# Down projection of a fused encoder block as seven half-size products, with tokens stationary and weight sums made in DRAM

## The chip, the core and the metric

The kernel runs on one core of a Trainium2 chip, alone. Its time is the device time of one execution in microseconds (us), as the median of several runs. A core has five engines that each work through their own list of instructions in order: TensorE (PE, matmuls, with its weight loads shown as PEld), VectorE (DVE), ScalarE (ACT), GpSimd (POOL) and SyncE (SP, which here only issues transfers). Engines wait for one another through semaphores. SBUF is the on-chip memory with 128 partitions, PSUM the accumulator memory that PE writes, in banks of 128 x 512 fp32 numbers; DRAM is reached by DMA alone, which 16 DMA engines carry out. DMAs are issued by SP, ACT or POOL, each on a queue of its own.

## The reference: what is computed

One encoder block for 512 tokens of width 1024, all in float32: three token mixers, a gated merge, an output projection, a convolutional gated feed-forward network and a last RMSNorm. The change touches the last two:

```
def rms_norm(x, g):
    y = x * rsqrt(mean(x * x, axis=-1) + EPS)
    return y * g

def conv_glu_ffn(h, w_up, w_conv, b_conv, w_down):
    a, u = split(h @ w_up, 2)                       # 512 x 2816 each
    return (gelu(dwconv3(a, w_conv, b_conv)) * u) @ w_down   # 2816 x 1024

x = x + merged @ w_out
x = x + conv_glu_ffn(rms_norm(x, ffn_norm_g), ...)
return rms_norm(x, final_norm_g)
```

The down projection is (512 x 2816) @ (2816 x 1024).

## The kernel before

**Numbers in two parts.** Each fp32 matrix is split into a high part h (rounded to the fp32r format by an ACT copy) and a rest l (a DVE subtraction). A product then is three matmuls into the same PSUM bank, `mm3` (L212): h·h, h·l and l·h. Activations are split by `split_act` (L217; ACT L219, DVE L220), weights by `emit_split` (L176; ACT L195, DVE L196).

**The weight stream.** All weights lie in one flat DRAM array in the order of use (`block_list`, L63), in blocks of up to 128 x 1024 numbers (512 KB). `weights(key)` (L201) issues the DMAs of blocks up to three ahead on SP (L159, three `raw` buffers) and the splits of blocks up to one ahead, in halves of at most 512 columns, into four `hi` and four `lo` buffers, and hands out the slices. A high half can be overwritten as soon as PE has used what was in its buffer; so an ACT copy L195 often waits for PE, and the rest L196 waits for it.

**Activations transposed.** Nearly all projections hold activations with features on partitions and tokens along the free axis: the weight slice of 128 x 128 is stationary, the 512 tokens move. `proj` (L409) computes one tile of 128 output features x 512 tokens with 8 x 3 matmuls. Some early projections (L524, and the memory values at L1061) have it the other way: 128 tokens are stationary and up to 512 weight columns move.

**Order.** A tile framework takes the program order as priority, places each engine's instructions statically and adds the semaphores. Between the stages of the big projections (`xaq`, `o`, `memk`, `memv`, `naq`, `nak`, then the merge gates) generators for the mixers are advanced by `step`; one of them raises row sums to the power -1/2 on POOL (L756), which DVE needs at once (L759). From the merge gates on, POOL issues window loads for the neighbourhood attention (L552). `late` holds work that the next `proj` emits after its second k (`flush`, L404).

**The feed-forward part** runs in two halves of 11 feature tiles each (L1296). For each feature tile f: `proj` of the gate part `ua` (48 matmuls for `ua` and `uu` together), `conv` (L466: DVE L470, ACT L472, DVE L473 and L474), gelu (ACT L1320, DVE L1321, ACT L1322, DVE L1323, POOL L1324), `proj` of `uu`, their product on DVE (L1327, which waits for POOL), and its split into two parts (L1328). After each half the down projection adds its share to the residual `x2` (features on partitions): 8 tiles of 11 x 3 matmuls of 512 tokens in the first half, with a DVE add out of PSUM (L1334). The second half has five such tiles; in its last tiles (`last_tiles`, L1166) the remaining work is ordered so that the norm of the first 256 tokens, of token tile 2 and of token tile 3 can be finished one behind the other: tiles of 256 tokens, then two products with tokens stationary over the last 256 features, with small fp32 matmuls and transposes between them. The norm's sums are taken over partitions with matmuls against ones. The results leave in three outputs (`outa`, transposed; `outb`; `outc`), which the host puts together.

Of the kernel before, what the change touches and what calls it, by code (L numbers as in the profile page):

```python
# [26 lines left out]
LF = KT - 2  # L27
# [34 lines left out]

def block_list():  # L63
# [35 lines left out]
for _i, (_k, _n) in enumerate(BLOCKS):  # L99
    BINDEX[_k] = (_i, _off, _n)  # L100
    _off += P * _n
WTOTAL = _off
BCOLS = {n: (lambda k: P) for n in ("mlk", "o", "xaq", "memk", "naq", "nak", "g", "out", "ua", "uu", "dn")}
BCOLS.update({n: (lambda k: 512) for n in ("mlq", "memv")})
BCOLS["tm"] = lambda k: TMC[k[1]]
BCOLS["br"] = lambda k: 256
BCOLS["dnl"] = lambda k: 256
# [3 lines left out]
def hybrid_block(ctx, tc, xg, xT, memT, wflat, vecs, gbias, nabias, outa, outb, outc):  # L111
# [33 lines left out]

    raws, split = {}, {}
# [3 lines left out]
    def emit_raw(i):  # L150
# [7 lines left out]
        src = wflat[off:off + P * n].rearrange("(p n) -> p n", p=P)  # L158
        SY.dma_start(r[:, :n], src)  # L159
# [6 lines left out]

    lw = []

    def lastw(k, m):

        if not lw:
            lw.extend(unit(F32R) for _ in range(4))
        q = slice(k % 8 * 256, k % 8 * 256 + m)
        return lw[k // 8][:, HI256:][:, q], lw[2 + k // 8][:, q]

    def emit_split(i):  # L176
# [4 lines left out]
        for a, b in hs:  # L181
            m = (b - a) * c
            if key[0] == "dnl":
                h, l = lastw(4 * key[1] + a, m)
            else:
                h = wp.tile([P, HWT], F32R, tag="hi", name=nm("wh"), bufs=4)
                l = wp.tile([P, HWT], F32R, tag="lo", name=nm("wl"), bufs=4)
                if key[:2] == ("tm", 2):
                    h = h[:, HI256:]
# [34 lines left out]
    gbf = cp.tile([P, 272], F32, name="gbf")  # L224
    gb, gfin = gbf[:, :16], gbf[:, 16:]
# [234 lines left out]
    SY.dma_start(gbf, gbias.partition_broadcast(P))  # L460
# [572 lines left out]
    for f in range(4):  # L1033
# [12 lines left out]
        V.tensor_scalar(so[0][:, f * S:(f + 1) * S], t, 1.0, None, op0=ALU.add)  # L1046
        step(RB)
    mkv = unit()
    mk, mv = mkv[:, 0:1024], mkv[:, 1024:2048]
    for f in range(4):  # L1050
        ps = proj(("memk", f), MH, ML, M)
        V.tensor_tensor(mk[:, f * M:(f + 1) * M], ps[:, :M], mrb, op=ALU.mult)
        step(RM)
    pss = [mmps() for _ in range(2)]
    for i in range(4):
        ws = weights(("memv", i))
# [10 lines left out]
    for f in range(4):  # L1067
        ps = proj(("naq", f), XH, XL)
        V.tensor_tensor(nq[:, f * S:(f + 1) * S].rearrange("p (b r c) -> p b r c", r=ROWS, b=4), rv(ps), rv(rb),
                        op=ALU.mult)  # L1070
        step(RB)
    for f in range(4):
        ps = proj(("nak", f), XH, XL)
        V.scalar_tensor_tensor(nk[:, f * S:(f + 1) * S], ps, 0.125, rb, op0=ALU.mult, op1=ALU.mult)
        step(RB)
# [79 lines left out]
    acc3 = cp.tile([P, S], F32, name="acc_3", tag="acc", bufs=1)  # L1155
    x2v = [u[:, :4 * S].rearrange("p (f s) -> p f s", f=4) for u in x2u]

    Hf = S // 2
    half = {}

    def power(v):
        col = tiny(v.shape[-1])
        G.tensor_tensor(col, v, nhalf[:, :v.shape[-1]], op=ALU.pow)
        return col

    def last_tiles(U, UL_):  # L1166

        ws = [w for i in range(3) for w in weights(("dnl", i))]  # L1170
        w5 = weights(("dn", 1, LF - 1, 0)) + weights(("dn", 1, LF - 1, 1))

        def half_tile(f, cs, at={}):
            ps = mmps()[:, :Hf]
            fs = slice((f - LF) * P, (f - LF + 1) * P) if f >= LF else slice(0, P)
            for k in range(HF):
                w = ws[k] if f >= LF else w5[k]
                mm3(ps, w[0][:, fs], w[1][:, fs], U[k][:, cs], UL_[k][:, cs], k == 0, k == HF - 1)
                if k in at:
                    at[k]()  # L1180
            xf = x2[f][:, cs]
            V.tensor_tensor(xf, ps, xf, op=ALU.add)
            sq = scr(Hf)
            A.activation(sq, xf, AF.Square)
            V.tensor_tensor(acc3[:, cs], acc3[:, cs], sq, op=ALU.add)
            A.activation(xf, xf, AF.Copy, scale=vcol("fin_g", f))

        for f in range(LF - 1, KT):
            half_tile(f, slice(0, Hf))

        def cols_a():
            ps = atps()
            for t in range(2):
                PE.matmul(ps[:, t:t + 1], acc3[:, t * P:(t + 1) * P], ones[:, 0:1], start=True, stop=True)
            v = tiny(2)
            V.tensor_scalar(v, ps[:, :2], 1.0 / D, EPS, op0=ALU.mult, op1=ALU.add)
            col = power(v)
            half["d"] = scr(Hf)
            for t in range(2):
# [259 lines left out]
```

## Time and profile before

| | |
|---|---|
| time, median of 3 runs | 878.68 us (878.55 to 878.86) |
| span of the profiled execution, first to last instruction | 877.0 us |
| time beside that span (median less span) | 1.7 us |
| PE busy | 871.5 us, 4330 matmuls |
| DVE busy | 582.3 us |
| ACT busy | 456.4 us |
| POOL busy | 126.5 us |
| DMA | 99.81 MB, mean 114 GB/s |

The profile gives no time for its own execution beside the span; the times are those of the three runs. In its timeline each line has the start in us from the span's start, the length, the engine, the line of the kernel, the operation, `out<-in` by tile names, partitions x elements, the count of merged instructions, and in brackets the time that the engine sat idle before it and what ended that. In a table of groups the last parts are busy us, mean ns of one, and the idle time before. The mean of 384 to 393 ns of a 128x512 matmul is its latency; matmuls overlap, so the pace is read from the distance of their starts.

### The profile page before, as it was taken

What the parts mean: (1) busy time and instruction counts of PE and PEld (TensorE: products, weight loads), DVE (VectorE), ACT (ScalarE), POOL (GpSimd) and SP (SyncE); (2) the same over time, 40 slices, a digit from 0 to 9 for tenths busy, and PEclk for the clock granted to TensorE, in tenths of its full rate; (3) what the DMA queues carried; (4) which work ended last, traced back from release to release, by engine and by line L of the source; (5) the groups of instructions that cost most, each with busy time, mean ns of one, the idle gap of its engine ahead of it and who ended that gap; (6) DMA issues with size and microseconds to landing.
All of it is one profiled execution on the core that took longest, in us unless ns stands there. A gap on an engine that the chain in (4) does not pass through costs nothing.

```text
span 877.0 us, 12216 instructions
## 1 busy us (share of the span) xinstructions
PE 871.5 (99%) x4330; PEld 739.1 (84%) x4330; DVE 582.3 (66%) x1195; ACT 456.4 (52%) x957; POOL 126.5 (14%) x202
## 2 busy tenths in 40 slices
PE   9999999999999999999999999999999999999997
PEld 7898889888888888888888888888888888888897
DVE  7694687775667758897676558677633466666433
ACT  7363557654456658888544454444422344444442
POOL 0101100001072470700000002111100011111011
PEclk9999999999999999999999999999999999999999
DMA  8324643522253453533233432322233323222412
GB/s 280 99 73 141 207 134 115 175 88 93 72 134 88 105 151 126 157 112 128 97 97 109 144 108 81 112 97 96 76 99 105 105 98 98 97 97 87 141 35 96
DMA packets 39421, 99.81 MB, mean 114 GB/s; under 512 B 5688, under 2 KB 13880, under 8 KB 39360
## 3 DMA queue, kind: packets, MB, share of 16 engines
q1 hardware_dynamic: 31568, 92.32, 32.0%
q0 software_dynamic: 7360, 6.32, 3.7%
q8 instruction: 34, 0.56, 0.3%
q10 hardware_dynamic: 432, 0.39, 0.1%
q14 instruction: 27, 0.22, 0.1%
HBM read 94.80 MB, written 4.21 MB: 113 GB/s over the span
## 4 chain that ended last, share of the span: by engine, by line
PE 99%; issue 0%; ACT 0%; DVE 0%; POOLq 0%; POOL 0%; DVEq 0%
PE mm L213 29%; PE mm L215 29%; PE mm L214 29%; PE at L214 2%; PE at L213 2%; PE at L215 2%; PE at L886 1%; PE at L739 1%; PE at L867 1%; PE at L704 1%; PE at L741 1%; PE at L848 0%; PE at L849 0%; PE at L720 0%; PE at L974 0%
## 5 line engine op out<-in xcount | busy, mean ns | idle before, releaser
L213 PE MATMUL mm<-u,wh 128*128 128x512 f32 (+1 forms) x1072 | 415.4, 387 | 0.0
L215 PE MATMUL mm<-u,wl 128*128 128x512 f32 (+1 forms) x1072 | 412.0, 384 | 0.0
L214 PE MATMUL mm<-u,wh 128*128 128x512 f32 (+1 forms) x1072 | 411.7, 384 | 0.0
L195 ACT ACTIVATE wh<-wr 128x512 fp32r<-128x512 f32 (+2 forms) x298 | 183.8, 621 | 229.1 <-PE mm L214 180.8
L196 DVE TENSOR_TENSOR wl<-wr,wh 128x512 fp32r<-128x512 f32 (+3 forms) x300 | 204.1, 682 | 93.3 <-ACT wh L195 87.0
L215 PEld LDWEIGHTS mm<-u,wl 128*128 128x128 f32 x1072 | 201.4, 188 | 40.1 <-DVE wl L196 0.2
L213 PEld LDWEIGHTS mm<-u,wh 128*128 128x128 f32 x1072 | 201.5, 188 | 38.7 <-ACT wh L195 0.5
L214 PEld LDWEIGHTS mm<-u,wh 128*128 128x128 f32 x1072 | 201.6, 188 | 38.6
L1324 POOL TENSOR_TENSOR s<-s,rb 128x512 f32<-128x512 f32 x22 | 38.6, 1757 | 403.1 <-DVE s L1323 403.1
L552 POOL DMA_DIRECT2D u<-nav_d x128 | 62.3, 519 | 66.4 <-PE at L886 23.1
L219 ACT ACTIVATE u<-s 128x512 fp32r<-128x512 f32 x26 | 16.4, 631 | 58.1 <-DVE s L1327 56.7
L1327 DVE TENSOR_TENSOR s<-mm,s 128x512 f32<-128x512 f32 x22 | 15.2, 690 | 23.7 <-POOL s L1324 23.7
L472 ACT ACTIVATE s<-pad,vec 128x512 f32<-128x512 f32 x30 | 24.4, 813 | 10.1 <-DVE pad L470 10.1
L220 DVE SCALAR_TENSOR_TENSOR u<-s,u 128x512 fp32r<-128x512 f32 x26 | 19.1, 733 | 14.7 <-ACT u L219 14.7
L473 DVE SCALAR_TENSOR_TENSOR s<-pad,vec,s 128x512 f32<-128x512 f32 x30 | 22.5, 750 | 5.6 <-ACT s L472 5.5
L1323 DVE SCALAR_TENSOR_TENSOR s<-s,s 128x512 f32<-128x512 f32 x22 | 15.2, 691 | 14.0 <-ACT s L1322 14.0
L474 DVE SCALAR_TENSOR_TENSOR s<-pad,vec,s 128x512 f32<-128x512 f32 x30 | 22.5, 751 | 0.9
L1322 ACT ACTIVATE s<-s 128x512 f32<-128x512 f32 x22 | 13.9, 632 | 15.5 <-DVE s L1321 15.4
L470 DVE TENSOR_TENSOR pad<-mm,rb 128x512 f32<-128x512 f32 x22 | 15.1, 690 | 6.2 <-PE mm L215 6.2
L213 PE MATMUL mm<-wh,u 128*128 128x512 f32 x48 | 18.9, 394 | 0.0
L215 PE MATMUL mm<-wh,u 128*128 128x512 f32 x48 | 18.7, 390 | 0.0
L214 PE MATMUL mm<-wl,u 128*128 128x512 f32 x48 | 18.7, 390 | 0.0
(317 smaller groups left out, 1012.1 us busy)
## 6 DMA issues: line engine op xcount, KB each, us to landing
wr<-wflat SPq DMA_DIRECT2D x141, 512.0 KB, 3.4
nab<-nabias SPq DMA_DIRECT2D x16, 256.0 KB, 2.7
u<-nav_d POOLq DMA_DIRECT2D x128, 32.0 KB, 2.8
s<-xT SPq DMA_DIRECT2D x15, 256.0 KB, 4.1
wr<-wflat SPq DMA_DIRECT2D x14, 192.0 KB, 2.3
nav_d<-nv POOLq DMA_DIRECT2D x8, 256.0 KB, 2.6
R<-rd SPq DMA_DIRECT2D x8, 256.0 KB, 3.7
wr<-wflat SPq DMA_DIRECT2D x2, 544.0 KB, 3.4
```

Source lines behind the costliest of these rows:

```text
L195: A.activation(h[:, u:v], src, AF.Copy)
L196: V.tensor_tensor(l[:, u:v], src, h[:, u:v].bitcast(F32), op=ALU.subtract)
L213: PE.matmul(ps, lh, rh, start=start, stop=False)
L214: PE.matmul(ps, lh, rl, start=False, stop=False)
L215: st["mm"] = PE.matmul(ps, ll, rh, start=False, stop=stop).ins
L219: A.activation(h, src, AF.Copy, scale=scale)
L220: V.scalar_tensor_tensor(l, src, scale, h.bitcast(F32), op0=ALU.mult, op1=ALU.subtract)
L472: A.activation(t1, pad[:, 0:512], AF.Identity, scale=vcol(w, i), bias=vcol(b, i))
L473: V.scalar_tensor_tensor(t1, pad[:, 1:513], vcol(w, n + i), t1, op0=ALU.mult, op1=ALU.add)
L474: V.scalar_tensor_tensor(t1, pad[:, 2:514], vcol(w, 2 * n + i), t1, op0=ALU.mult, op1=ALU.add)
L552: G.dma_start(vw[r * 32:(r + 1) * 32, i * 256:(i + 1) * 256], nav_v[hf, r, CW[b]:CW[b] + 32, hp * 256:(hp + 1) * 256])
L1324: G.tensor_tensor(c, c, rb2, op=ALU.mult)
```

## The change

The down projection of both halves is regarded as a 2 x 2 block product: tokens in two halves, hidden features in two halves (the two halves of the up projection), output features in two halves. It is computed by the Winograd form of Strassen's scheme, with seven products of half size (256 tokens x 1408 x 512) for eight. Operands are sums and differences:

- Weight sums `T1` to `T4` (each 1408 x 512 fp32) are built in DRAM by eight DMAs (`sum_steps`): two copies issued by ACT, two further copies and four accumulating DMAs issued by POOL. They are placed with `next(sums)` between the projections `o` and `nak`, two of them in `memk` and `memv`.
- Activation sums are built on POOL in the up stages: one half-size subtraction per tile in the first half, three operations in the second. Their splits go to `late`, or are made while an earlier product runs (`slices`).
- Each product (`product`) holds 128 tokens stationary and lets 512 weight columns move; weights come in blocks of two k (`dn` with 1024 columns), used by two token tiles, so 12 matmuls per block. Two products accumulate onto a bank pair that an earlier product left in PSUM (`T2` and `T4` onto `B11`'s; `B22` onto `T1`'s).
- The first half now runs products `B11` and `T3`, the second `B21`, `T2`, `T1`, `T4`, `B22`. A list says what DVE, ACT and POOL do beside which block of them.
- The residual is turned to tokens by rows: `turn`, eight times four PE transposes and an ACT copy, in the first half's up stage. `gather` adds banks to it on DVE (128 x 512 each).
- The norm is taken by tokens: squares with row sums on ACT, the gain multiplied on POOL (`gain`, 128 x 512) with a `final_norm_g` broadcast to all partitions, the power on POOL, the scaling on ACT (`finish`). In the last product the last three k of the second token tile are held back to the end (`hold=3`). There is one output, tokens by rows.

```diff
-        for f in range(8 if hh == 0 else LF):
-            if hh == 1 and f >= LF - 3:
-                i = f - LF + 3
-                L.append((("dnl", i), 256 * (4 if i < 2 else 3)))
-            for i, n in ((0, 8), (1, 3)):
-                L.append((("dn", hh, f, i), n * 128))
+        for p in PRODUCTS[hh]:
+            for i in range(HB):
+                L.append((("dn", p, i), min(2, HF - 2 * i) * 512))
...
+    def sum_steps():
+        for d, n in (("T1", "B11"), ("T3", "B12")):
+            A.dma_start(wide(wsum[d]), wide(quarter(n)))
+            yield
+        for d, n in (("T1", "B12"), ("T3", "B22")):
+            G.dma_start(wide(wsum[d]), wide(quarter(n)), accum_op=ALU.add, max_dma_last_dim=8192)
+            yield
+        for d, n, m in (("T2", "T1", "B22"), ("T4", "T2", "B21")):
+            G.dma_start(wide(wsum[d]), wide(quarter(n)))
+            yield
+            G.dma_start(wide(wsum[d]), wide(quarter(m)), accum_op=ALU.add, max_dma_last_dim=8192)
+            yield
...
+    def turn(g):
+        t, f = g % NT, g // NT
+        pt = atps()
+        for i in range(4):
+            PE.transpose(pt[:, i * P:(i + 1) * P], x2[4 * f + i][:, t * P:(t + 1) * P], ident)
+        A.activation(cv(t, f), pt, AF.Copy)
...
+    def product(name, ab, banks, first, hold=0, then={}):
+        ah, al = ab
+        ws = []
+        for i in range(HB):
+            ws += weights(("dn", name, i))
+            if i == 0:
+                flush()
+            for g in then.get(i, ()):
+                g()
+            for k in range(2 * i, len(ws)):
+                for t in range(2):
+                    if k < HF - hold or t == 0:
+                        tile_mm(ah[k], al[k], ws[k], banks[t], t, first and k == 0)
+        for k in range(HF - hold, HF):
+            tile_mm(ah[k], al[k], ws[k], banks[1], 1, first and k == 0)
+
+    def tile_mm(ah, al, w, bank, t, start):
+        ts = slice(t * P, (t + 1) * P)
+        PE.matmul(bank, ah[:, ts], w[0], start=start, stop=False, skip_group_check=True)
+        PE.matmul(bank, ah[:, ts], w[1], start=False, stop=False, skip_group_check=True)
+        PE.matmul(bank, al[:, ts], w[0], start=False, stop=True, skip_group_check=True)
+
+    def gather(banks, a, f, op):
+        for t in range(2):
+            c = cv(2 * a + t, f)
+            V.tensor_tensor(c, c, banks[t], op=op)
...
+    def gain(t, f):
+        G.tensor_tensor(cv(t, f), cv(t, f), gfin[:, f * S:(f + 1) * S], op=ALU.mult)
...
-            V.tensor_tensor(c, pu, c, op=ALU.mult)
-            split_act(UH[j], UL[j], c, 0.5)
...
+            V.tensor_tensor(r, pu, c, op=ALU.mult)
+            if hh == 0:
+                split_act(a11[0][j], a11[1][j], r[:, one_], 0.5)
+                G.tensor_tensor(r[:, one_], r[:, one_], r[:, two_], op=ALU.subtract)
+                late.append(lambda j=j, r=r: split_act(s3[0][j], s3[1][j], r[:, one_], 0.5))
+            else:
+                q = r0[j]
+                split_act(a12[0][j], a12[1][j], r[:, one_], 0.5)
+                G.tensor_tensor(q[:, two_], q[:, two_], r[:, two_], op=ALU.subtract)
+                late.append(lambda j=j, q=q: split_act(s1[0][j], s1[1][j], q[:, two_], 0.5))
+                G.tensor_tensor(q[:, one_], q[:, one_], r[:, two_], op=ALU.add)
+                G.tensor_tensor(r[:, one_], r[:, one_], q[:, one_], op=ALU.subtract)
+        if hh == 0:
+            pa_, pd = [atps() for _ in range(2)], [mmps() for _ in range(2)]
+            product("B11", a11, pa_, True)
+            product("T3", s3, pd, True, then={0: [lambda: gather(pa_, 0, 0, ALU.add)]})
+            late.append(lambda b=pd: (gather(b, 1, 0, ALU.add), gather(b, 1, 1, ALU.subtract)))
...
+    product("B21", a12, pd, True, then=slices(s2, r0, one_, -0.5))
+    a22 = parts()
+    product("T2", s2, pa_, False, then=at(slices(a22, r1, two_, 0.5, 1), 1, lambda: gather(pd, 0, 0, ALU.add),
+                                          lambda: ready(0, 0, 1)))
+    s4 = parts()
+    product("T1", s1, pc, True, then=at(slices(s4, r1, one_, 0.5, 1), 0, lambda: gather(pa_, 0, 1, ALU.subtract),
+                                        lambda: gather(pa_, 1, 1, ALU.subtract)))
+    product("T4", a22, pa_, False, then={0: [lambda: gather(pc, 1, 1, ALU.add), lambda: ready(1, 2, 3)]})
+    product("B22", s4, pc, False, hold=3, then={0: [lambda: gather(pa_, 1, 0, ALU.add), lambda: ready(0, 2, 3),
+                                                    lambda: finish(2), lambda: finish(3)]})
```

`ready(f, *ts)` takes `squares` and `gain` of the token tiles ts. After the last product come the two last gathers, the squares and the gain of token tile 0 and its `finish`, then the square, the power and four scalings of token tile 1, and its two stores of 256 KB. The function `last_tiles` is gone.

More of the change, by code (lines that the diff above doesn't have):

```diff
@@ L26 @@
 HF = FT // 2
-LF = KT - 2
+HB = (HF + 1) // 2
+Hf = S // 2
 NU = 15
@@ L143, in atps @@
         return atp.tile([P, 512], F32, tag="at", name=nm("at"))
+    wsum = {n: dp.tile([QSIZE], F32, name=f"wsum_{n}") for n in ("T1", "T2", "T3", "T4")}
+    wide = lambda a: a.rearrange("(p n) -> p n", n=1024)
+    quarter = lambda n: wsum[n] if n in wsum else wflat[QOFF[n]:QOFF[n] + QSIZE]
+    def sum_steps():
[10 more added lines that the diff above has]
+            yield
+    sums = sum_steps()
     raws, split = {}, {}
@@ L1046, in hybrid_block @@
         V.tensor_scalar(so[0][:, f * S:(f + 1) * S], t, 1.0, None, op0=ALU.add)
+        if f % 2:
+            next(sums)
         step(RB)
@@ L1052, in hybrid_block @@
         V.tensor_tensor(mk[:, f * M:(f + 1) * M], ps[:, :M], mrb, op=ALU.mult)
+        if f == 1:
+            next(sums)
         step(RM)
@@ L1055, in hybrid_block @@
     for i in range(4):
+        if i == 1:
+            next(sums)
         ws = weights(("memv", i))
@@ L1070, in hybrid_block @@
                         op=ALU.mult)
+        if f % 3 == 0:
+            next(sums)
         step(RB)
@@ L1074, in hybrid_block @@
         V.scalar_tensor_tensor(nk[:, f * S:(f + 1) * S], ps, 0.125, rb, op0=ALU.mult, op1=ALU.mult)
+        if f % 2:
+            next(sums)
         step(RB)
@@ new lines, in ready, with at @@
+    def ready(f, *ts):
+        for t in ts:
+            squares(t, f)
+            gain(t, f)
+    def at(d, i, *fs):
+        d.setdefault(i, []).extend(fs)
+        return d
+    product("B21", a12, pd, True, then=slices(s2, r0, one_, -0.5))
[5 more added lines that the diff above has]
+                                        lambda: gather(pa_, 1, 1, ALU.subtract)))
```

265 lines of the change are left out of this document (92 added, 173 removed).

## The prediction

> **What bounds the kernel now.** I read the page first, then the table of busy time by stage, then the timeline of the down projection and of the places the change touches.
>
> ```profile
> span 877.0 us, 12216 instructions
> PE 871.5 (99%) x4330; PEld 739.1 (84%) x4330; DVE 582.3 (66%) x1195; ACT 456.4 (52%) x957; POOL 126.5 (14%) x202
> ...
> PE 99%; issue 0%; ACT 0%; DVE 0%; POOLq 0%; POOL 0%; DVEq 0%
> ```
>
> TensorE (PE) is busy 99% of the span and is 99% of the chain that ended last. So a matmul that is left out shortens the kernel by its slot, as long as nothing else then makes PE wait. The stages that matter, by the table of windows (columns: window, length, busy us and count of each engine, granted clock, DMA share, GB/s):
>
> ```profile
> core 0: us, PE busy (x) PEld busy (x) DVE busy (x) ACT busy (x) POOL busy (x), PEclk, DMA share, GB/s
> 160.00:171.50 11.50, 11.50 (x64) 9.84 (x63) 8.21 (x21) 7.79 (x22) 0.00 (x0) 1.00 0.62 207
> ...
> 808.10:845.50 37.40, 37.40 (x166) 30.97 (x165) 17.69 (x28) 17.26 (x30) 5.68 (x4) 1.00 0.33 113
> 845.50:871.60 26.10, 26.04 (x218) 25.77 (x217) 9.93 (x29) 6.12 (x14) 3.12 (x4) 1.00 0.14 47
> ```
>
> PE has no gap in either part of the second down projection, at full clock, while VectorE (DVE) is busy less than half of it. The slot of a matmul comes from the DVE adds that take up each finished down tile:
>
> ```profile
> 636.27 0.69 DVE L1334 TENSOR_TENSOR u<-mm,u 128x512 f32<-128x512 f32 x1 [1.08 <-PE mm L215]
> 643.75 0.69 DVE L1334 TENSOR_TENSOR u<-mm,u 128x512 f32<-128x512 f32 x1 [1.15 <-PE mm L215]
> ...
> 845.71 0.69 DVE L1334 TENSOR_TENSOR u<-mm,u 128x512 f32<-128x512 f32 x1 [1.15 <-PE mm L215]
> ```
>
> One tile is 33 matmuls and takes 643.75 − 636.27 = 7.48 us: 0.2267 us for 512 columns. A measurement of this kernel can tell about 0.2% (1.8 us) from no change. The span is 877.0 us and the median 878.68, so 1.7 us lie around the span; the sum below is for the span, and 1.7 us are added at the end.
>
> **The change, term by term.**
>
> *Fewer matmuls.* Before, the first half's eight tiles take 8 × 7.48 = 59.8 us, the second half's five full tiles 37.4, and the rest runs from the add at 845.71 to the ScalarE (ACT) square at 871.77 (below), both of which start 0.2 us behind the matmul they wait for: 26.1 us. Together 123.3 us. After, there are seven products of 11 (k) × 2 (token tiles) × 3 = 66 matmuls of 512 columns: 462 × 0.2267 = 104.7 us. Saved: 18.6 us. Loops are unrolled, so the counts are certain; that the change doesn't do what it says is no case here.
>
> *Tokens stationary.* The memory-value projection (L1061) already holds tokens stationary, with blocks of the same size and the same 12 matmuls per block as the new products:
>
> ```profile
> 167.35 0.40 PE L214 MATMUL mm<-wl,u 128*128 128x512 f32 x1
> ...
> 172.38 0.39 PE L215 MATMUL mm<-wh,u 128*128 128x512 f32 x1
> ```
>
> The 22 slots between them take 5.03 us, 0.2286 each. At worst 462 × 0.0019 = 0.9 us, at best nothing; I take 0.3, because these rows follow small matmuls, behind which slots are a little long anyway.
>
> *Transposes.* The residual x2 is turned to tokens by rows: eight `turn`s of four transposes in the first up stage, where PE has no gap to hide them.
>
> ```profile
> 254.59 1.03 PE L974 MATMUL at<-ident,s 128*128 128x128 f32 x8
> 255.38 0.48 PE L213 MATMUL mm<-u,wh 128*128 128x512 f32 x1
> 255.70 0.39 PE L214 MATMUL mm<-u,wh 128*128 128x512 f32 x1
> ```
>
> Without the eight transposes the L214 matmul would have come at 254.59 + 0.23 = 254.82; it comes at 255.70, so eight cost 0.88 us and thirty-two 3.5; with eight separate interruptions I take 3.6. Their copies out of PSUM go on ACT, 52% busy.
>
> *The end.*
>
> ```profile
> 871.57 0.60 PE L1239 MATMUL at<-ident,u 128*128 128x128 f32 x4
> 871.77 0.39 ACT L1273 ACTIVATE s<-mm 128x257 f32<-128x257 f32 x1 [3.88 <-PE mm L215]
> ...
> 872.05 0.19 ACT L1273 ACTIVATION_READ_ACCUMULATOR s<-mm 128x1 f32 x1
> ...
> 872.32 0.54 POOL L1163 TENSOR_TENSOR y<-y,nhalf 128x1 f32<-128x1 f32 x1 [3.55 <-ACT s L1273]
> ...
> 872.89 0.35 DVE L1277 TENSOR_SCALAR s<-s,y 128x256 f32<-128x256 f32 x1 [1.18 <-POOL y L1163]
> 873.16 0.48 DVE L1281 SCALAR_TENSOR_TENSOR s<-mm,y,gbf 128x256 f32<-128x256 f32 x1
> ...
> 873.76 0.35 ACTq L1283 DMA_DIRECT2D outb<-s  x1
> ```
>
> Before, the last product ends at 871.57, and 5.4 us later the span is over, 3.2 of them after the last DMA is issued at 873.76. After, a DVE add (0.2 + 0.69) comes ahead of the square, the square is 512 wide (about 0.6 + 0.19), then a small DVE add (0.2 with its handover), the power on GpSimd (POOL, 0.54 + 0.1), three DVE scalings in a row (0.35, 0.48, 0.48 less overlap: 1.2), the issue (0.1) and the same 3.2: 7.1 us, so 1.7 more. Bounds: no more than now if the held-back matmuls (`hold=3`) cover the add, and 4 more if token tile 0's two ACT scalings stand ahead of the square and its 512 KB store competes with the last two.
>
> *The up stages.* The loop of one feature tile on DVE sets how far DVE can lag:
>
> ```profile
> 578.46 0.69 DVE L1327 TENSOR_TENSOR s<-mm,s 128x512 f32<-128x512 f32 x1 [1.19 <-POOL s L1324]
> ...
> 588.75 0.69 DVE L1327 TENSOR_TENSOR s<-mm,s 128x512 f32<-128x512 f32 x1 [1.19 <-POOL s L1324]
> ...
> 726.71 0.69 DVE L470 TENSOR_TENSOR pad<-mm,rb 128x512 f32<-128x512 f32 x1 [0.38 <-PE mm L215]
> ```
>
> DVE's own loop is 10.29 us against 48 × 0.2267 = 10.88 of PE; early on DVE is behind and catches up, later it waits 0.38 for PE. A half-size split costs DVE half of a full one, so two of them cost what one did:
>
> ```profile
> 863.42 2.43 DVE L1210 TENSOR_TENSOR u<-u,s 128x256 f32<-128x256 f32 x7
> ...
> 170.38 1.29 DVE L196 TENSOR_TENSOR wl<-wr,wh 128x512 fp32r<-128x512 f32 x2 [0.99 <-ACT wh L195]
> ```
>
> 0.35 us for 256 columns, 0.65 for 512. New on POOL: one half-size subtraction per tile in the first up stage, three in the second. They meet DVE on SBUF:
>
> ```profile
> 533.30 1.82 POOL L1324 TENSOR_TENSOR s<-s,rb 128x512 f32<-128x512 f32 x1 [164.37 <-DVE s L1323]
> ...
> 533.86 1.81 DVE L196 TENSOR_TENSOR wl<-wr,wh 128x512 fp32r<-128x512 f32 x1
> ...
> L1341 POOL TENSOR_TENSOR acc<-acc,s 128x512 f32<-128x512 f32 x4 | 5.2, 1293 | 32.7 <-ACT s L1340 32.7
> ```
>
> The weight split that began at 533.86, inside POOL's operation, took 1.81 us instead of 0.65 and ended 0.55 after POOL did: it was shut out. [...]
>
> A half-size POOL operation is about 1.29 / 2 = 0.65 us. Three per tile shut DVE out for 0 (when they fall into DVE's own waits) to 1.95 us. I take 1.0, as DVE waits 1.19 and 0.7 of each loop anyway, less 0.25 for the shorter wait on ACT: a loop of about 11.0, 0.15 over PE's, so DVE falls back 1.6 us in eleven tiles. It starts 2.4 us behind (four `gather`s of 512 columns). Before, a lag of about 8 × (10.88 − 10.29) = 4.7 us in the first up stage left PE without a gap. I allow 1.0 us of PE waits; bounds 0 and (12.0 − 10.88) × 11 + 2.4 − 4.7 = 10.
>
> *The products.* A weight block now serves 256 tokens and not 512, so splits double: 11 per 14.96 us. The fullest product is T1: 11 × 0.65 for weights, 11 × 0.35 for the next operand, four gathers of 0.65: 13.6 us of 14.96 on DVE. ACT has 11 × 0.57 twice at most. The six POOL `gain`s before the end shut DVE out for at most 1.29 each, in products with two gathers. Each fits; I allow 0.5 us.
>
> *The weight sums* (128 x 512 x 11 numbers, 2.88 MB each; four copies, four accumulations) are issued here:
>
> ```profile
> L1036 DVE TENSOR_TENSOR s<-mm,rb_x x4: 680/684/692, 127.0 to 143.0; 128x512 f32<-128x512 f32 x4
> ...
> L1052 DVE TENSOR_TENSOR u<-mm,rb_m x4: 416/418/419, 150.0 to 159.9; 128x256 f32<-128x256 f32 x4
> ...
> L1069 DVE TENSOR_TENSOR u<-mm,rb_x x4: 691/691/692, 179.8 to 201.0; 128x512 f32<-128x512 f32 x4
> ...
> L1074 DVE SCALAR_TENSOR_TENSOR u<-mm,rb_x x4: 682/691/692, 209.1 to 229.2; 128x512 f32<-128x512 f32 x4
> ...
> L756 POOL TENSOR_TENSOR y<-y,nhalf 128x4 f32<-128x4 f32 x4 | 4.1, 1033 | 91.4 <-DVE y L754 91.4
> L759 DVE TENSOR_SCALAR H<-H,y 128x128 f32<-128x128 f32 x16 | 3.9, 351 | 3.8 <-POOL y L756 3.8
> ```
>
> By these rows T1 is copied near 132 and summed near 153, T2 copied at 180 and summed at 201, T4 copied at 216 and summed at 229; the results are read only after 640. Each POOL issue waits for the transfer before it, and behind it on POOL stand the powers of L756, whose reader L759 blocks DVE, and later the window loads of L552. No transfer from DRAM to DRAM is in this trace. From the window at 160, 207 GB/s at a share of 0.62 is 334 GB/s flat out: 8.6 us for 2.88 MB, 14 beside the weight stream. An accumulation reads two operands: 17 to 27 us. With 20 the chain is 5 us late at T4 alone, inside what PE rides out; I take nothing, bound 8 (with 27, T4's copy waits 12, of which 4 to 5 are ridden out). [...]
>
> **Sum:** −18.6 + 0.3 + 3.6 + 1.7 + 1.0 + 0.5 = −11.5. Span 865.5, time **867.2 us**.
>
> **Rivals.**
> *The vector engines become the bound* (faster, but less). For it: the 1.81 us row; POOL has three operations per tile and DVE little slack (0.38). Against: much of it falls into waits. The full lock gives 10 us in place of the 1.5 allowed: 876; halfway 871.
> *The weight stream starves in 150 to 172.* There one block of 512 KB is due every 2.7 us, 190 GB/s, while two accumulations run. With half of 334 GB/s left, 22 us stretch by an eighth (3 us: 870); with a third, 190 / 111 on eight blocks less two held ahead, about 10: 877. Against it: the stage lasts only 22 us.
> *POOL waits for the sums* (slower). If an accumulation takes 33 us, T2's copy waits 6 us on POOL and T4's 18; the powers, DVE's L759 and the window loads stand behind them, and PE loses about 16: 883. It decides from about 31 us on. Against it: the rates above. For it: DMAs between DRAM buffers are unpriced here, and POOL's order is fixed.
>
> **Chances.** The sum as it stands 0.60; vector bound 0.16; starving 0.07; POOL waits 0.12; several small losses that cancel the gain 0.05. Faster 0.82, same 0.05, slower 0.13. Range: from 863 (no stall, tail and slots as now: −18.6 + 3.6 = −15 gives 863.7) to 878, which takes in the bounds of the vector and starving cases and leaves out the slow one.
>
> **What would show it.** Right: PE at 99% with 0.227 us slots in all seven products, down stages of 29.9 and 74.8 us, 7 us from the last matmul to the end. Wrong: PE gaps behind weight splits in the second up stage or in T2 and T1, DVE operations of 1 us and more beside POOL's; POOL waiting on DMAs between 180 and 245 with gaps of PE behind L759; slots above 0.23.

## The result and the profile after

The kernel after takes **951.75 us** (median of 4 runs, 950.9 to 952.2) beside 878.71 us of the kernel before (878.55 to 878.86): a ratio of 1.083, 95% interval 1.0815 to 1.0846. It is slower by 73 us where 867.2 was forecast, far out of the range of 863 to 878. The profiled execution has a span of 950.1 us.

The page of the kernel after (columns as before):

```profile
span 950.1 us, 12184 instructions
PE 873.7 (92%) x4173; PEld 729.1 (77%) x4173; DVE 629.4 (66%) x1262; ACT 486.5 (51%) x1045; POOL 170.6 (18%) x255
...
PE   6245599999999999999999999999999999998995
...
PEclk9567699999999999999999999999999999999999
DMA  9998834544432424535333243232326323224563
...
HBM read 126.91 MB, written 27.28 MB: 162 GB/s over the span
...
PE 81%; DMA 10%; DVE 4%; ACT 2%; POOL 2%; issue 1%; SPq 0%; POOLq 0%; DVEq 0%; ACTq 0%
```

PE is on 81% of the chain and no longer 99%; DMA has come in with 10%. The slices say where: PE is idle half the time in the first five, about 119 us, at a time when the DMA engines are 9 tenths busy. The same by stage, with the columns of the table of windows (after first, then before):

```profile
0.00:113.00 113.00, 51.63 (x169) 37.50 (x170) 27.91 (x62) 22.85 (x40) 9.73 (x30) 0.70 0.92 258
113.00:600.00 487.00, 487.00 (x2533) 417.52 (x2532) 347.78 (x811) 289.01 (x676) 75.22 (x148) 1.00 0.40 124
600.00:706.00 106.00, 106.00 (x484) 87.72 (x484) 82.00 (x122) 53.58 (x97) 24.29 (x20) 1.00 0.28 95
706.00:737.00 31.00, 31.00 (x138) 25.45 (x137) 18.94 (x31) 15.02 (x26) 2.89 (x2) 1.00 0.56 179
737.00:856.00 119.00, 119.00 (x527) 98.47 (x525) 87.27 (x126) 51.86 (x93) 41.04 (x40) 1.00 0.29 96
856.00:942.00 86.00, 79.11 (x331) 62.43 (x329) 63.84 (x112) 51.68 (x109) 15.95 (x13) 0.98 0.52 168
```

```profile
0.00:36.00 36.00, 35.20 (x154) 28.27 (x155) 24.06 (x57) 20.77 (x37) 4.81 (x24) 1.00 0.59 201
```

After, PE runs 169 matmuls in the first 113 us; before, it ran 154 in 36. From 113 us on it is as full as it was, up to 856. The chain of waits of those first 113 us (start, length, what):

```profile
6.26 14.02 DMA wsum_T<-wflat
20.59 25.41 DMA wsum_T<-wflat
46.29 25.33 DMA wsum_T<-wsum_T
71.90 19.27 DMA wsum_T<-wflat
91.46 10.76 DMA wsum_T<-wsum_T
102.51 0.94 POOL wsum_T L170
103.44 1.10 POOL rc_x L338
```

These are the weight sums. They read nothing that the program computes, and the scheduler issued all eight at the very start and not where the program names them: ACT's copies at 6.3 and 8.3 us, POOL's six in a row, each waiting for a transfer that it builds on. Behind the sixth on POOL's queue stands `rc_x`, the power that the first normalisation needs. It and the first `conv` add of the feed-forward part (FFN) in both kernels, after first (count, shortest, median and longest in ns, first and last start in us):

```profile
L338 POOL TENSOR_TENSOR rc_x<-y,nhalf x1: 1396/1396/1396, 103.1 to 103.1; 128x4 f32<-128x4 f32 x1
L488 DVE TENSOR_TENSOR pad<-mm,rb x22: 679/684/694, 600.0 to 856.2; 128x512 f32<-128x512 f32 x22
```

```profile
L320 POOL TENSOR_TENSOR rc_x<-y,nhalf x1: 1030/1030/1030, 30.9 to 30.9; 128x4 f32<-128x4 f32 x1
L470 DVE TENSOR_TENSOR pad<-mm,rb x22: 676/693/695, 526.3 to 802.9; 128x512 f32<-128x512 f32 x22
```

The power starts 72.2 us later, the FFN 73.7 us later; from there to the end it is 350.1 us against 350.7. So there are two questions: what about the sums costs 73 us, and where are the 11.5 us that the FFN part was to gain?

### The profile page after: what moved, and what is told of

It reads as the page before. It is cut to its first block, busy times and chain, and to the rows that moved or that the text cites. A ratio compares the mean times of both kernels' runs of the same rounds, so it can differ in the third digit from the quotient of the medians.

```text
span 950.1 us, 12184 instructions
## 1 busy us (share of the span) xinstructions
PE 873.7 (92%) x4173; PEld 729.1 (77%) x4173; DVE 629.4 (66%) x1262; ACT 486.5 (51%) x1045; POOL 170.6 (18%) x255
## 3 DMA queue, kind: packets, MB, share of 16 engines
q0 software_dynamic: 8992, 23.62, 10.8%
## 4 chain that ended last, share of the span: by engine, by line
PE 81%; DMA 10%; DVE 4%; ACT 2%; POOL 2%; issue 1%; SPq 0%; POOLq 0%; DVEq 0%; ACTq 0%
PE mm L234 21%; PE mm L232 21%; PE mm L233 21%; DMA wsum_T<-wflat 6%; DMA wsum_T<-wsum_T 4%; PE at L1227 2%; PE at L1228 2%; PE at L1226 2%; DVE wl L215 1%; PE at L233 1%; PE at L232 1%; PE at L234 1%; PE mm L1227 1%; PE mm L1228 1%; PE mm L1226 1%
## 5 line engine op out<-in xcount | busy, mean ns | idle before, releaser
L232 PE MATMUL mm<-u,wh 128*128 128x512 f32 (+1 forms) x907 | 358.3, 395 | 37.3 <-ACT u L238 20.0
L233 PE MATMUL mm<-u,wh 128*128 128x512 f32 (+1 forms) x907 | 353.4, 390 | 1.1 <-DVE u L239 1.1
L234 PE MATMUL mm<-u,wl 128*128 128x512 f32 (+1 forms) x907 | 353.2, 389 | 0.0
L215 DVE TENSOR_TENSOR wl<-wr,wh 128x512 fp32r<-128x512 f32 (+2 forms) x335 | 243.0, 730 | 106.3 <-ACT wh L214 102.4
L232 PEld LDWEIGHTS mm<-u,wh 128*128 128x128 f32 x907 | 172.8, 191 | 72.0 <-ACT u L238 21.3
L233 PEld LDWEIGHTS mm<-u,wh 128*128 128x128 f32 x907 | 172.6, 190 | 36.0 <-DVE u L239 2.6
L234 PEld LDWEIGHTS mm<-u,wl 128*128 128x128 f32 x907 | 172.3, 190 | 35.6 <-DVE wl L215 0.8
L1226 PE MATMUL at<-wh,u 128*128 128x512 f32 x110 | 42.9, 390 | 1.6 <-ACT wh L214 1.6
L1227 PE MATMUL at<-wl,u 128*128 128x512 f32 x110 | 43.0, 391 | 0.2 <-DVE wl L215 0.2
L1228 PE MATMUL at<-wh,u 128*128 128x512 f32 x110 | 42.8, 389 | 0.0
L238 ACT ACTIVATE u<-r 128x256 fp32r<-128x256 f32 x44 | 17.7, 414 | 40.8 <-DVE r L1293 25.0
L239 DVE SCALAR_TENSOR_TENSOR u<-u,u 128x256 fp32r<-128x256 f32 (+1 forms) x42 | 22.5, 554 | 6.4 <-ACT u L238 6.3
L491 DVE SCALAR_TENSOR_TENSOR s<-pad,vec,s 128x512 f32<-128x512 f32 x30 | 22.9, 762 | 5.9 <-ACT s L490 5.8
L239 DVE SCALAR_TENSOR_TENSOR u<-r,u 128x256 fp32r<-128x256 f32 x44 | 21.8, 503 | 7.5 <-ACT u L238 7.5
## 6 DMA issues: line engine op xcount, KB each, us to landing
wsum_T<-wflat POOLq DMA_DIRECT2D x4, 2816.0 KB, 22.3
wsum_T<-wflat ACTq DMA_DIRECT2D x2, 2816.0 KB, 18.6
```

Source lines behind the costliest of these rows:

```text
L215: V.tensor_tensor(l[:, u:v], src, h[:, u:v].bitcast(F32), op=ALU.subtract)
L232: PE.matmul(ps, lh, rh, start=start, stop=False)
L233: PE.matmul(ps, lh, rl, start=False, stop=False)
L234: st["mm"] = PE.matmul(ps, ll, rh, start=False, stop=stop).ins
L238: A.activation(h, src, AF.Copy, scale=scale)
L239: V.scalar_tensor_tensor(l, src, scale, h.bitcast(F32), op0=ALU.mult, op1=ALU.subtract)
```

## Experiments

The first theory: POOL's order alone cost the 73.7 us, through the held-up power. Its rival: the traffic, 0.92 of the DMA engines, would cost as much at any place. Line numbers in the rows are those of the kernel named, a few off from kernel to kernel.

**e3_none: the floor.** T1 to T4 are read as four of the quarters, and nothing is summed.

```
-            src, off = (wsum[key[1]], off) if key[1] in wsum else (wflat, QOFF[key[1]] + off)
+            off += QOFF[dict(T1="B11", T2="B12", T3="B21", T4="B22").get(key[1], key[1])]
...
-            next(sums)
```

> No sums are made: T1 to T4 are read as the four quarters, so the output is not the reference's, while every matmul and weight load stays. It is the floor for any place of the sums. Main theory: 878 (951.75 - 73.7), so the rest of the change gains nothing by itself: what the 42 fewer weight tiles save is lost in the second up stage. My prediction's own account would give 867 here.

Measured: 879.0 us, ratio 1.0003 (0.9993 to 1.0012). All of the 73 us is the sums'; without them the change is worth nothing, and not 11.5 us.

**e1_places, e2_late: the same sums elsewhere.** An order edge (`issue_after`) keeps each behind an instruction of its engine.

```
-            next(sums)
+            with tc.issue_after(st["pool"]):      # e1: behind POOL's latest power
+                next(sums)
...
+        if f < 6:
+            with tc.issue_after(st["vw"]):        # e2: behind the last window load
+                next(sums)
```

> The eight sums are tied by order edges to where the program names them (the copies behind the o projections' tanh on ACT, POOL's six behind rc_m's power and the four norm powers of the mLSTM heads). Main theory (POOL's order held rc_x's power from 31 to 103 us, and that alone cost the 73.7 us by which the FFN began later): the power is back at 31 us and the time falls to about 878, since the FFN part took 350.1 us where it took 350.7 before. Rival, the traffic theory (the 92% full DMA engines cost it, wherever the transfers stand): weights are starved at 140 to 240 us instead and the time stays above 920. Rival, POOL waits (my third rival of the prediction): the norm powers stand behind transfers of 19 to 25 us each, so 885 to 900.

> The same sums put later: the two copies behind two tanh of the second branch's gates, POOL's six behind the last window load of the neighbourhood attention, where POOL has nothing until the first up product. Main theory: about 878, as with no sums at all. Traffic theory: above 900 with PE gaps in 370 to 530 us. If the six take over 160 us there, POOL's multiplication by rb2 in the first up tile comes late and it is 880 to 890.

Measured: 912.5 us (1.0371 to 1.0402) and 892.1 us (1.0143 to 1.0174). Neither pure theory holds: the first one's 878 fails at both places, and pure traffic fails too, since the same bytes cost 73, 34 and 13 us above the floor. The third number for e1, 885 to 900 by POOL's waits, fails as well: PE's longest gap there, 14.5 us at 156, comes from ACT, which stands 19.4 us for one load of `R`, while the readers of the powers wait 2.7 us in all. In e2_late PE's matmuls follow those of e3_none at one distance except at 413 to 434 us, where 12 us are lost. The chain ahead of that, and the row of that load in the view of its tile (least, median and longest from issue to landing; its 256 KB took 2.7 us at the median before):

```profile
400.17 25.08 DMA nab<-nabias
```

```profile
DMA to landing us min/median/max: 2.5/4.4/25.1
```

One small load took 25.1 us beside the sums. POOL holds nothing up here, so this is a second cause beside POOL's order.

**e4_behind_power: the sums behind `rc_x`'s power.**

```
+        st.setdefault("px", st["pool"])           # rc_x's power
...
+            with tc.issue_after(st["px"]):
                 next(sums)
```

> The sums stay at the start as the scheduler put them, only POOL's six come behind rc_x's power (and the small fills that belong to it), so the transfers still fill the first 110 us but hold back no computation of POOL's there. Main theory (blocking): most of the 73 us comes back, 880 to 905. Traffic theory: the weights are starved by the same bytes, 930 to 950.

Measured: 930.4 us (1.0564 to 1.0599), at the low end of the traffic theory's range. But it isn't the bytes alone: with `rc_x` out of the way the wait moves to the next instruction behind POOL's sums: the store of `nav_d` is issued at 133 us and then takes 17.8 us, and PE has a gap of 30 us. Another 17.6 us are lost by 32 us, where the load of `vec` takes 22 us. So it doesn't separate the two.

**e11_copies_first, e5_ffn_sums: only the copies at the start, then nothing.** In e11 ACT's two copies are where the scheduler had them and POOL's six stand in the up stages, 23 to 62 us apart; in e5 all eight do, 19 to 62 us apart. Both sum T3 ahead of T1.

```
+            st["up"] = G.tensor_tensor(c, c, rb2, op=ALU.mult).ins
+            if f in SUM_AT:                       # 0, 3, 5, 8, 11, 13, 16, 18 in e5
+                with tc.issue_after(st["gelu"]), tc.issue_after(st["up"]):
+                    next(sums)
```

> ACT's two copies stand at the start, where the scheduler put them in the kernel after; POOL's six sums are in the up stages, where they cost nothing. It prices the two copies alone, with POOL's order untouched: in the run with the sums behind rc_x's power PE lost 17.6 us in its first 20 us, with the load of vec landing after 22.3 us. If that was the copies' doing, 895 to 899; if POOL's order or the sums behind it had a part in it, 880 to 885.

> The sums alone are moved again, into the up stages: one of the eight every 23 to 34 us, each behind the gelu's tanh (ACT's two copies) or behind the multiplication by rb2 (POOL's six) of up tiles 0, 3, 5, 8, 11, 13, 16 and 18. Traffic theory as it now stands (a sum of 2816 KB holds back whatever small transfer is wanted within its 12 to 25 us; weights that are asked for three blocks ahead are not): there is no such small transfer in the up stages, and 878 to 881 comes out, the floor without sums (879.0). If the weights themselves are starved by the sums' bytes, PE gaps appear at 560 to 740 us and it is 890 or more.

Measured: e11 895.9 us (1.0173 to 1.0221), e5 879.6 us (1.0003 to 1.0022), each as its first theory had it. In the up stages all the sums together cost nothing beside the floor, though they fill the DMA engines there to two thirds. The first up stage of e5:

```profile
526.00:633.00 107.00, 107.00 (x489) 88.53 (x488) 80.78 (x123) 54.07 (x98) 25.95 (x22) 1.00 0.68 194
```

The share is 0.68 instead of 0.28, and PE is busy for 107.00 of 107 us. Weights that are asked for three blocks ahead stand that. The two copies alone at the start cost 895.9 − 879.0 = 17 us, and this is the chain there (the same 86 KB took 5.7 us in e5):

```profile
5.08 23.11 DMA vec<-vecs
```

Adding POOL's six behind them, as the scheduler did, costs another 951.75 − 895.9 = 56 us. In this order of adding, that is how the 73 us are made up.

**e12_late_2k, e13_fine, e14_fine_behind, e15_fine_places: smaller pieces.** In the traces a plain copy is 64 pieces of 11264 numbers (45 KB) and an adding one 352 of 2048 (8 KB). All are cut to 1408 pieces of 512 numbers (2 KB; POOL's two plain copies went as 704 of 4 KB), at the places of e2, of the kernel after, of e4 and of e1:

```
-            A.dma_start(wide(wsum[d]), wide(quarter(n)))
+            A.dma_start(wide(wsum[d]), wide(quarter(n)), max_dma_last_dim=2048)
...
-            G.dma_start(wide(wsum[d]), wide(quarter(n)), accum_op=ALU.add, max_dma_last_dim=8192)
+            G.dma_start(wide(wsum[d]), wide(quarter(n)), accum_op=ALU.add, max_dma_last_dim=2048)
```

> The sums at the late places that gave 892.1, only cut finer: the plain copies went as 64 pieces of 11264 numbers (45 KB) and the adding ones as 352 of 2048; now all are 1408 pieces of 512 numbers (2 KB). The same bytes at the same places. Piece theory (a load of 256 KB took 25.1 us instead of 4.4 because its small pieces stood behind 45 KB ones in each engine): the wait goes, 879 to 882. Traffic theory (bytes alone): 890 to 894, or more as small pieces move slower and POOL needs longer to issue them.

> The kernel after, every sum at the place where the scheduler put it, cut into 2 KB pieces only. POOL's order is as it was, so rc_x's power still waits for six steps that wait for one another (about 85 to 100 us at 12 to 24 us each). Order theory (the power is the most of it): 935 to 955, hardly less than 951.75. Piece theory (loads held behind 45 KB pieces are the most of it): 895 to 915.

> The same cut with POOL's sums behind rc_x's power (930.4 with large pieces, of which 17 us came from the two copies in the first 20 us and 33 us at about 105 us, where nav_d's write stood behind POOL's last sum and then took 17.8 us). The first part is by pieces and should go; of the second the waiting on POOL's queue stays. 905 to 915 if so; 880 to 890 if all of it was pieces.

> The same cut at the places that the program names (912.5 with large pieces). What remains is POOL's order alone: the four norm powers of the mLSTM heads behind sums that wait for one another. Piece theory: 880 to 890. Order theory: 900 to 912.

Measured: 880.7 (1.0015 to 1.0036), 957.2 (1.0879 to 1.0911), 936.1 (1.0637 to 1.0675) and 904.1 us (1.0276 to 1.031). The piece theory holds at e2's place; at e1's the order theory does, at the start e13 is even above its range, and e14 missed both of its ranges. At the late place the cut takes away 11.4 of 13 us, and the load of `nab` is back at

```profile
DMA to landing us min/median/max: 2.5/5.3/7.1
```

Same bytes, same place: what held that load was the size of the pieces beside it, not the traffic. The trace's record of the pieces shows how. POOL's queue (q0, the sums) above SP's (q1, the loads), with pieces, MB and share of the 16 engines' time, in e2_late at 404 to 408 us beside an adding sum, there at 417 to 421 beside a copy, and in e12 at 404 to 408:

```profile
q0 software_dynamic: 89, 0.73, 87.3%
q1 hardware_dynamic: 92, 0.19, 14.0%
...
q0 software_dynamic: 35, 1.58, 98.5%
q1 hardware_dynamic: 33, 0.07, 4.8%
...
q0 software_dynamic: 234, 0.48, 64.3%
q1 hardware_dynamic: 230, 0.63, 44.6%
```

Each time both queues move about as many pieces; the loads' pieces have 2 or 4 KB, and the larger the sum's, the fewer bytes are left for the loads. The load of 25.1 us met both sizes: until 416 us SP's queue was still at the two loads issued before it, beside pieces of 8 KB, and only its own pieces went beside those of 45 KB.

Where POOL's order decides, the cut doesn't help, it costs 5 to 6 us (an accumulation takes 25.1 us instead of 22.3 at the median, from issue to landing). PE's waits of e13 in its first 120 us (line waited for, sum, times, longest):

```profile
PE at L371 <- DVE s L362: 58.6, 1, 58.6
PE mm L232 <- ACT u L238: 10.0, 2, 9.1
PE mm L232 <- ACT wh L214: 1.9, 1, 1.9
```

and the same three of the kernel after in its first 113:

```profile
PE at L371 <- DVE s L362: 22.2, 1, 22.2
PE mm L232 <- ACT u L238: 20.0, 3, 7.9
PE mm L232 <- ACT wh L214: 17.3, 1, 17.3
```

The waits for ACT, which stands for loads, fall from 37 to 12 us, and PE comes earlier to the wait for `rc_x` (L362 reads what comes of it), where it stands for longer: two delays side by side, of which the longer counts. The 39 us that PE waits in e14 are again for `nav_d`: its store follows the sums on POOL's queue and takes 17.7 us, as it took 17.8 in e4, so small pieces don't help there. Nor are the copies at the start free in small pieces. By 34 us PE of e14 is 12 us behind e3_none, where e4 was 17.6 behind, and the reason is another wait. SP issues a load of `s` from `xT` only when a copy has landed, and ACT then waits 10.7 us for it:

```profile
SPq L254 <- DMA wsum_T<-wflat: 13.5, 1, 13.5
```

The same wait of SP is 11.1 us in the kernel after and in e11, and absent in e3_none; what ties that load to the copy was not traced. So not all of the 17 us of the copies come from the size of pieces. In e15 POOL stands 36 us before the adding halves of T2 and T4, and the norm powers with it:

```profile
POOL wsum_T L170 <- DMA wsum_T<-wsum_T: 35.8, 2, 22.6
...
DVE H L777 <- POOL y L774: 16.3, 4, 13.6
```

This is the mechanism of the prediction's third rival; PE has a gap of 11 us by it at 247 us, and 6.5 us are lost before, at 156 to 178. The program's own places would have cost 25 us with small pieces and 34 with large ones.

**e6_two_less: where the 11.5 us went.** On the floor without sums, two of POOL's three operations per tile of the second up stage are left out too.

```
-                G.tensor_tensor(q[:, one_], q[:, one_], r[:, two_], op=ALU.add)
-                G.tensor_tensor(r[:, one_], r[:, one_], q[:, one_], op=ALU.subtract)
```

> On the floor without sums (T1 to T4 read as quarters) two of POOL's three operations per tile of the second up stage are left out too (q += r2 and r -= q, so s2 and s4 hold other numbers; the output is not the reference's). Lock theory (POOL's operations stretch VectorE's beside them, VectorE falls behind by 0.54 us a tile, and PE pays when the second down stage begins): the gaps of 7.9 us at 782 to 805 vanish, 870 to 872. If VectorE's own operations set the lag, 878 as before.

Measured: 872.9 us (0.9916 to 0.9946), 6.1 under the floor, 0.9 over the lock theory's range and far from its rival's 878. The groups of the second up stage, kernel after first, e6 below (busy us, mean ns of one):

```profile
L215 DVE TENSOR_TENSOR wl<-wr,wh 128x512 fp32r<-128x512 f32 x42 | 34.1, 812 | 0.3 <-ACT wh L214 0.2
...
L1301 POOL TENSOR_TENSOR r<-r,u 128x256 f32<-128x256 f32 x10 | 7.4, 738 | 8.0 <-DVE u L1293 8.0
...
L239 DVE SCALAR_TENSOR_TENSOR u<-r,u 128x256 fp32r<-128x256 f32 x10 | 6.8, 678 | 2.0 <-ACT u L238 2.0
```

```profile
L215 DVE TENSOR_TENSOR wl<-wr,wh 128x512 fp32r<-128x512 f32 x45 | 31.0, 690 | 2.3 <-ACT wh L214 0.8
...
L239 DVE SCALAR_TENSOR_TENSOR u<-r,u 128x256 fp32r<-128x256 f32 x14 | 5.8, 423 | 2.0 <-ACT u L238 2.0
```

A weight split takes 812 ns beside three POOL operations and 690 beside one; an operand split 678 and 423. DVE's loop is 11.42 us (the adds L488 at 753.4 to 844.8, eight tiles) against PE's 10.88; in e6 the same adds are 10.88 us apart. So DVE falls 0.54 us a tile behind, and PE pays when the second down stage begins. PE's waits at 855 to 877 in the kernel after:

```profile
PEld mm L1227 <- DVE wl L215: 5.7, 5, 1.8
PE mm L1227 <- DVE wl L215: 3.8, 4, 1.5
```

**e7_reorder, e8_both: POOL's operations moved behind the up stage.** Eleven beside B21 and eleven beside T2, with the products as B21, T1, T2, T4, B22; e7 without sums, e8 with those of e5.

```
+        with tc.issue_after(st["up"]):
+            G.tensor_tensor(d, d, e, op=op)
...
-PRODUCTS = (("B11", "T3"), ("B21", "T2", "T1", "T4", "B22"))
+PRODUCTS = (("B11", "T3"), ("B21", "T1", "T2", "T4", "B22"))
```

> On the same floor, nothing left out but the sums: the two POOL operations per tile are tied behind the up stage (11 beside B21, 11 beside T2), the products run as B21, T1, T2, T4, B22, so that s2 and s4 are needed later, and the scaling of rows 256 to 511 (finish) stands three blocks later in B22. Lock theory: the lag is gone at the start of B21, and the two bursts of 11 stretch VectorE where it has room (a weight split of 0.68 for 1.36 us of PE): 868 to 872. If the lock only moves along with the operations, 876 to 879. The gap of about 2.5 us at 857 should go in any case (its ACT copies waited for POOL's gains ahead of the weight splits).

> The whole kernel with both: sums in the up stages as in the first run of this set, products and POOL operations as in the third. By the theories that those two test it is the sum of both, 868 to 874, under the kernel before; if either of them fails, at most as far above as that one.

Measured: 884.3 (1.0055 to 1.0085) and 885.2 us (1.0058 to 1.0088). Both missed, by more than either theory allowed. The lock moved along: the groups of e7 from 784 to 796 us, in the first burst,

```profile
L1329 POOL TENSOR_TENSOR r<-r,u 128x256 f32<-128x256 f32 x11 | 9.7, 913 | 0.0
...
L215 DVE TENSOR_TENSOR wl<-wr,wh 128x512 fp32r<-128x512 f32 x3 | 3.5, 1178 | 0.0
```

Eleven POOL operations back to back make a weight split 1178 ns long, just where PE needs one every 1.36 us and DVE is behind. By the starts of its matmuls (what they lie apart beyond 0.227 us, a halved clock included, which in the kernel after is 0.50 at 871 to 874) PE loses 5.4 us here, where e3_none loses 6.7 at the start of B21. It loses 6.0 us beside the second burst at 811 to 823, and 4.4 at 841 to 846, where T4, by the new order, accumulates onto banks that DVE has yet to gather. So the bursts are only a part of what this order costs.

**e9_shifted, e10_hi5: DVE's work moved instead.** POOL's three operations stay. Beside B21 DVE has only weight splits; the operand splits come in T1, T2 and T4, the gathers one to a block, T4 has its own banks, `finish` of rows 256 to 511 stands three blocks later; the sums as in e5. In e10 the high halves have five buffers too.

```
+    product("B21", a12, pd, True)
+    product("T1", s1, pc, True, then=spread(slices(s2, r0, one_, -0.5), (1, lambda: part(pd, 0, 0, ALU.add, 0)),
...
+        with tc.issue_after(st["wl"]):            # behind the latest weight split
+            split_act(ab[0][j], ab[1][j], src, scale)
```

> The whole kernel again, sums in the up stages, POOL's three operations per tile left in the second up stage as the change has them. What moves is VectorE's work of the second down stage: products in the order B21, T1, T2, T4, B22, so that beside B21 VectorE has only the weight splits (11 x 0.68 = 7.5 us in B21's 15 us of PE) and can take up the 6 us by which it lags; the splits of s2, a22 and s4 are tied behind weight splits of T1, T2 and T4; T4 has a bank pair of its own, the gathers stand one to a block, and the scaling of rows 256 to 511 three to four blocks into B22. Lag theory (the cost of the lock is paid only because s2's splits come right behind the lag): the 7.9 us at the start of B21 and the 2.5 to 4 us in B22 go, 868 to 872. If the lag itself is what PE waits for (a12's last tiles), 3 to 4 us remain there and it is 873 to 876.

> As the run before with a fifth buffer for the high halves of split weights (the low halves keep four, there is no room for both). If PE's short waits come from ACT's halves being late, 1 to 3 us less than that run; if from VectorE's low halves, the same within 1 us.

Measured: e9 **875.25 us**, ratio 0.996 (0.9946 to 0.9974), 0.4% faster than the kernel before; e10 879.7 us (1.0003 to 1.0022), which neither of its two theories allowed. Counted as above, in e9 the waits of B22 are gone (about 4 us in e5), and at B21's start 5.8 us of e5's 7.2 are left, so the outcome is the second of the two named: PE waits for the last tile's own chain through DVE, ACT and POOL. e10 loses 3.8 of its 4.5 us in the first down stage, with waits for DVE's low halves (3.4 us) that e9 doesn't have there; why ACT's extra buffer brings them was not traced.

## Why the prediction was wrong, term by term

- **The weight sums, 0 with a bound of 8: this step failed.** They cost 73 us. The prediction placed each issue "near 132 … 153 … 229" by the line that the program names, and so asked only what waits near there. An instruction that depends on nothing has no such place; the scheduler put all eight at the start. Its third rival had the right mechanism, POOL's queue waiting for the sums, but at the wrong place, with the wrong victim (the norm powers in place of `rc_x`) and with "POOL's order is fixed", which was taken from the program. The rates were nearly right for the accumulations: 19 and 25 us in the chain above where 17 to 27 was given; of the copies one took 25 us where 8.6 to 14 was.
- What the prediction left out altogether is that a load which PE needs soon can be held by a large transfer: 12 us by one 256 KB load in e2_late, through the size of the sums' pieces, and 17 us by the two copies alone, of which the pieces explain a part.
- **Fewer matmuls, −18.6: right.** The first two products take 30.1 us (706.1 to 736.2) where 29.9 was given; the other five take 85.5 (855.9 to 941.4), 10.7 over the 74.8 forecast, and 10.5 of that are gaps and slow slots between the starts of matmuls.
- **Tokens stationary, +0.3: right.** The first two products hardly have a gap (0.1 us), and their 132 slots took 0.2 us more than at 0.2267 each.
- **Transposes, +3.6: right.** A tile with a turn takes PE 11.36 us in place of 10.88, eight times 0.48: 3.8.
- **The end, +1.7: 3.3.** From the last product's end to the span's it is 8.7 us in place of 5.4. The chain shows what was not counted, token tile 0's `gain` ahead of token tile 1's power on POOL:

```profile
941.10 1.28 POOL u L1244
942.38 0.51 POOL y L1251
```

- **The up stages, +1.0 with bounds 0 and 10: the mechanism right, the size not.** A loop of 11.42 us came where 11.0 was estimated and 12.0 was the bound. PE lost about 8.3 us by it at the start of B21, 1.5 of them at a halved clock (0.50 at 871 to 874 us). The value was taken near the wrong end, as most of the lock was expected to fall into DVE's waits; and a half-size POOL operation took 738 to 925 ns where 650 was reckoned.
- **The products, +0.5: about 2.4.** ACT's scaling in `finish` waits 2.7 us for the power, which stands behind the gains on POOL, and the weight splits stand behind that scaling on ACT; e9 takes that away.

The FFN terms as measured: −18.6 + 3.8 + 0.2 + 10.7 + 3.3 = −0.6, which is the 350.1 us in place of 350.7; the floor of 879.0 is 0.3 above the kernel before, the same within what can be told. Of that part the vector rival (871 to 876, chance 0.16) had the true mechanism, though its times were too low. The starving of 150 to 172 us could not show in the kernel after, since no sum ran there.

## What to carry to other kernels

Ask of every operation that a change adds whether anything holds it back; if not, look for it at the start of the program, ahead of what its engine does there, and tie it with an order edge to the place that was meant. Long transfers belong into a stage whose own loads are asked for well ahead (879.6 us in e5 beside 951.75), on a queue on which nothing urgent stands behind them (the store of `nav_d` took 17.8 us in e4); where a small load may be wanted beside them, cut them into small pieces (at most 7.1 us for a load of `nab` in e12, 25.1 in e2_late), which themselves take longer (25.1 us for an accumulation in e13, 22.3 in the kernel after). And where an engine runs at its limit, count the operations that another engine runs beside it at their full price (a weight split of 812 ns beside three POOL operations a tile, 690 beside one). Here it paid to move the work that was due later, and not to move the neighbour's operations.

## What the runs showed of the hardware

- Beside each other the DMA queues moved like numbers of pieces and not like bytes: in e2_late 35 and 33 pieces in 4 us, but 1.58 and 0.07 MB. In what order an engine takes the pieces of its queues the trace doesn't show. In the kernel after a piece of 45 KB took 1.9 us at the median, an adding piece of 8 KB 0.63, a 4 KB piece of a load 0.16. Beside copies in 45 KB pieces the load of `vec` (86 KB) took 23.1 us in e11, and 5.7 in e5, where no sum ran at that time.
- A DRAM-to-DRAM copy of 2816 KB took 10.8 to 25.3 us in the kernel after and 11.5 and 11.6 in e2_late, where ACT's two stand apart (from issue to landing); an accumulation 18.3 to 30.1 in the kernel after. Its pieces went there at about half a copy's rate: 8 KB added in 0.63 us are 13 GB/s for an engine, 45 KB copied in 1.67 us, the shortest, are 27. That an accumulation takes twice a copy's time (17 to 27 us beside 8.6 to 14) was an estimate in the prediction.
- Granted PE clock: in the first 113 us of the kernel after, with PE idle half the time, it was 0.70; at 108 to 113 us, behind the longest gap, it was 0.50, and matmuls lay 0.43 us apart in place of 0.23. Part of the lost time is this.
